# A hybrid diffusion layer on one core: tokens by quarters behind the heads, experts chosen during the merges, a regrouped gate matrix, and half of v split ahead

## The chip, the core and the metric

The kernel is one program on one core of a Trainium2 chip. The metric is the device time of one execution in microseconds, median of several runs. A core has TensorE (matmuls, PE in the profile; PEld its weight loads), VectorE (DVE), ScalarE (ACT), GpSimd (POOL) and SyncE (SP). Each works through its own instructions in order. DMAs are issued from the queues of SP, ACT and GpSimd and are carried by 16 shared DMA engines.

## What is computed

A layer over 1024 latent tokens and 256 context tokens of width 1024: two bidirectional gated linear scans (8 HGRN2 heads, 4 GLA heads) with one input projection, a gated merge of the two, an output projection, and then PEER, a retrieval of 16 out of 16384 experts per token for each of 8 heads. Cut to what the change touches:

```python
y = sigmoid(m_hg) * y_hg + sigmoid(m_gla) * y_gla
x = x + mod[2] * (y @ w_o)
h = modulate(rmsnorm(x, norm_ffn_g), mod[3], mod[4])
q  = (h @ wq).reshape(-1, 8, 2, 128)
s1 = einsum("nhd,kd->nhk", q[:, :, 0], k1); s2 = einsum("nhd,kd->nhk", q[:, :, 1], k2)
v1, i1 = top_k(s1, 16); v2, i2 = top_k(s2, 16)
top_s, top_c = top_k(v1[..., :, None] + v2[..., None, :], 16)
expert = i1[top_c // 16] * 128 + i2[top_c % 16]
act = gelu(einsum("pd,ped->pe", h, u[expert]))
x = x + mod[5] * einsum("pe,ped->pd", softmax(top_s) * act, v[expert])
return rmsnorm(x, final_g)
```

## The kernel before

Large products are made exact to about fp32 with two fp16 halves per operand: `split` (L91) writes the high half on ACT (L93) and the low half on DVE (L94), and `mm3` (L100) multiplies high by high, high by low and low by high. `ld` is a DMA on SP's queue, `st_` one on ACT's. The instructions' order on each engine is set by the order of the program text, in which generators are advanced by hand, and by a scheduler that moves loads ahead as far as their buffers allow.

*Heads* (to about 1460 us). Twelve heads are projected and scanned; the weight slabs come through three buffers (`w32`) that `slab` (L174) loads and splits. Beside them `presplit` (L311) splits weights of later stages and stores them in DRAM: 16 slabs of the two branch projections, 8 of the output projection, 16 of the query projection. `meanwhile` (L331) advances it by `PRE` = 0.25 units per 512 projected tokens. The merge gates (`w_m`) and the modulations (`mw`) come last.

*Merges* (1460 to about 1880). For each half of the tokens, 8 steps (`merge_step`, L818) multiply both branches by their weights, gate and add them (the addition on GpSimd) and split the result; `out_proj` (L833) gives x1, and `next_norm` (L871) normalises and transposes it into `hb`. In the second half's steps the generator `choosing(0)` (L764) is advanced by the table `CS`: `scores` (L739) multiplies by the query weights and the keys on PE, and DVE searches the best 16 (`top16`) of 128 twice per token block and head and then of 64 sums.

*Gating part* (1880 to 2858). Five token blocks (`DB` = 2, 3, 5, 6, 7) take the dense way: `route` turns the choice into expert numbers and gates on DVE, `gate_block` (L1051) builds for 4 tokens at a time one-hot matrices on DVE, multiplies them on PE and copies the result by ACT into `gs`; each 32 tokens the gate matrix `G_d` gets a store. The planner's price of each piece is what the generators yield (1.65 per 4 tokens, 16.0 a routing, 3.3 and 1.5 in choosing). Whenever the sum passes `U_US` = 6.2, `early_tile` (L1101) multiplies one tile of 128 experts' u with the dense tokens (transposes, `ph`), and stores the activations in `act_d`; 80 of 128 tiles are early. Each early tile also issues `G_E` = 3.4 gathers: the other three blocks (`GB` = 0, 1, 4) fetch their 128 chosen rows of u and then of v by indirect DMA from GpSimd (L940), and DVE uses each (L919, L924), 768 in all, six held in flight. They start once two blocks are routed, which `prep` does first.

*Expert loop* (to 4180). 32 groups of 4 expert tiles: the group's gates are loaded (`gt4`), activations are loaded or computed (`u_act`), `weigh` multiplies and splits them, `v_tile` (L1144) loads and splits v, and `out_unit` (L1151) multiplies for each of the five blocks; DVE adds the product to `acc` (L1162). The gathers left are fed in evenly. Then comes the final norm.

## Time and profile before

| | us |
|---|---|
| runs shown (3), lowest, median, highest | 4216.97, 4217.43, 4219.64 |
| profiled execution, its own time | 4229.67 |
| its span, first to last instruction | 4228.0 |
| PE busy (matmuls) | 3884.8 (92%) |
| DVE busy | 2938.6 (70%) |
| ACT busy | 1430.1 (34%) |
| GpSimd busy | 1683.9 (40%) |
| DMA, mean rate | 209 GB/s |

Busy time is the time in which at least one instruction of the engine ran; matmuls are pipelined, so a group's mean duration is longer than the distance between two of them. The granted clock is TensorE's, as a share of full speed. The idle time before an instruction is put down to what released it last.

### The profile page before, as it was taken

The numbers are of one execution on the slowest core, as the hardware profiler recorded it, in microseconds if no ns is written. First come the engines' busy times: TensorE is split into PE (matmuls) and PEld (weight loads), VectorE is DVE, ScalarE is ACT, GpSimd is POOL, SyncE is SP. The second block draws the span as 40 slices with busy tenths as digits, with TensorE's granted clock in tenths as the row PEclk, the third lists the DMA queues.
The fourth block names the chain that finished last, engine by engine and source line by source line (L and its number), as shares of the span: only waits on it lengthen the run. The fifth ranks groups of instructions, "written<-read, shape, count | busy, mean of one in ns | idle before, by whom it ended". The sixth has DMA issues, their size and how long they took to land.

```text
span 4228.0 us, 60334 instructions
## 1 busy us (share of the span) xinstructions
PE 3884.8 (92%) x23802; PEld 2350.2 (56%) x23802; DVE 2938.6 (70%) x5132; ACT 1430.1 (34%) x2194; POOL 1683.9 (40%) x1197
## 2 busy tenths in 40 slices
PE   6999999999999999988999989986899989999997
PEld 2665665656655444445776667763445544444453
DVE  5345446242556414379987799977989999889998
ACT  5344444243343202034543334552222222222222
POOL 2011111010011012127655567635766666666663
PEclk9999999999999999999999999987999999999998
DMA  5222122221223583227887778869989999989996
GB/s 189 78 73 85 56 73 79 74 87 46 87 64 115 162 282 107 99 97 242 295 307 249 254 242 298 305 228 319 329 318 336 321 323 325 316 311 325 328 315 232
DMA packets 435306, 884.64 MB, mean 209 GB/s; under 512 B 28511, under 2 KB 245066, under 8 KB 431438
## 3 DMA queue, kind: packets, MB, share of 16 engines
q0 software_dynamic: 110592, 402.70, 27.3%
q1 hardware_dynamic: 202676, 320.19, 22.6%
q10 hardware_dynamic: 121754, 157.89, 10.6%
q8 instruction: 186, 3.05, 0.3%
q14 instruction: 98, 0.80, 0.1%
HBM read 764.80 MB, written 115.88 MB: 208 GB/s over the span
## 4 chain that ended last, share of the span: by engine, by line
PE 47%; DVE 25%; DMA 11%; issue 8%; ACT 6%; POOL 4%; SPq 0%; ACTq 0%; DVEq 0%; POOLq 0%
PE ph L100 5%; DVE row_False L919 5%; PE pe L100 5%; DVE gacc L924 4%; PE pgm L1065 3%; PE pq L100 3%; PE pj_f0h L100 3%; PE pv_g L100 2%; PE pv_h L100 2%; DMA row_False<-in_peer_u_dram,idx 2%; PE pj_f1h L100 2%; PE pj_m L100 2%; DMA vn<-in_peer_v_dram 2%; DMA acr<-act_d 2%; PE pso L100 2%
## 5 line engine op out<-in xcount | busy, mean ns | idle before, releaser
L100 PE MATMUL pe<-v,w 128*128 128x512 f16 x3840 | 883.8, 392 | 138.7 <-DVE acc L1162 104.7
L100 PE MATMUL ph<-hb,uT 128*128 128x256 f16 (+1 forms) x6144 | 892.2, 303 | 14.6 <-POOL uT L967 10.4
L100 PEld LDWEIGHTS <-uT 128*128 128x128 f16 x6144 | 609.4, 99 | 242.5 <-POOL uT L967 13.1
L100 PEld LDWEIGHTS <-w 128*128 128x128 f16 x3840 | 384.0, 100 | 623.0 <-issue 166.4
L940 POOL DMA_INDIRECT row_False<-in_peer_u_dram,idx x384 | 548.9, 1429 | 274.6 <-DVE row_False L919 169.2
L940 POOL DMA_INDIRECT row_True<-in_peer_v_dram,idx x384 | 503.6, 1311 | 264.1 <-DVE gacc L924 173.1
L924 DVE SCALAR_TENSOR_TENSOR gacc<-row_True,dots,gacc 128x1024 f32<-128x1024 f32 x381 | 539.7, 1416 | 39.4 <-DMA row_True<-in_peer_v_dram,idx 35.8
L919 DVE SCALAR_TENSOR_TENSOR row_False<-row_False,h2n 128x1024 f32<-128x1024 f32 x384 | 496.2, 1326 | 67.1 <-DMA row_False<-in_peer_u_dram,idx 66.7
L967 POOL TENSOR_TENSOR uT<-uf,uT 128x512 f16<-128x512 f32 x256 | 380.8, 1499 | 284.0 <-ACT uf L966 282.6
L93 ACT ACTIVATE v<-vn 128x1024 f16<-128x1024 f32 x128 | 135.1, 1055 | 501.9 <-DMA vn<-in_peer_v_dram 386.7
L979 ACT ACTIVATE ac<-ph 128x256 f32<-128x256 f32 (+1 forms) x256 | 110.1, 438 | 371.8 <-PE ph L100 367.1
L1065 PE MATMUL pgm<-oh 128*128 128x128 f16 x1280 | 176.4, 295 | 53.2 <-ACT gs L1066 38.8
L1066 ACT ACTIVATE gs<-pgm 128x512 f32<-128x512 f32 x160 | 171.0, 1069 | 136.6 <-PE pgm L1065 136.6
L94 DVE SCALAR_TENSOR_TENSOR v<-vn,v 128x1024 f16<-128x1024 f32 x128 | 168.2, 1314 | 50.5 <-ACT v L93 50.3
L1162 DVE TENSOR_TENSOR acc<-pe,acc 128x1024 f32<-128x1024 f32 x155 | 188.6, 1217 | 11.8 <-PE pe L100 11.7
L100 PE MATMUL pj_m<-hb,w_m 128*128 128x512 f16 x768 | 187.4, 401 | 2.3 <-DVE lf_g L86 1.6
L1065 PEld LDWEIGHTS <-oh 128*128 128x128 f16 x1280 | 145.7, 117 | 77.0 <-issue 63.5
L100 PE MATMUL pq<-hb,w_wq 128*128 128x512 f16 x768 | 180.0, 387 | 1.0 <-POOL hb L89 0.8
L964 ACT ACTIVATE uT<-put 128x512 f16<-128x512 f32 x256 | 155.0, 605 | 71.0 <-PE put L961 69.4
L89 DVE TENSOR_TENSOR oh<-iota,rTr 128x1024 f16<-128x1024 f16 x160 | 139.1, 879 | 33.9 <-PE pgm L1065 33.8
L100 PEld LDWEIGHTS <-hb 128*128 128x128 f16 x1536 | 150.2, 98 | 17.8 <-issue 0.3
L966 ACT ACTIVATE uf<-put 128x512 f32<-128x512 f32 x256 | 154.4, 603 | 8.9 <-POOL uT L967 8.8
(364 smaller groups left out, 5531.9 us busy)
## 6 DMA issues: line engine op xcount, KB each, us to landing
un<-in_peer_u_dram SPq DMA_DIRECT2D x128, 512.0 KB
vn<-in_peer_v_dram SPq DMA_DIRECT2D x128, 512.0 KB
G_d<-gs ACTq DMA_DIRECT2D x20, 2048.0 KB
gt<-G_d ACTq DMA_DIRECT2D x32, 1280.0 KB
act_d<-ac ACTq DMA_DIRECT2D x80, 320.0 KB
acr<-act_d SPq DMA_DIRECT2D x80, 320.0 KB
mw<-in_ada_w_dram SPq DMA_DIRECT2D x32, 512.0 KB
w_wq<-wq_d SPq DMA_DIRECT2D x32, 512.0 KB
```

The lines of the kernel that those rows point to most:

```text
L89: eng.tensor_tensor(out=out, in0=in0, in1=in1, op=op)
L94: return V.scalar_tensor_tensor(out=lo, in0=src, scalar=float(scale), in1=hi, op0=ALU.mult, op1=ALU.subtract)
L100: PE.matmul(ps, lhsT=a(k), rhs=b(k), start=n == 0, stop=n == last)
L919: V.scalar_tensor_tensor(out=row, in0=row, scalar=1.0, in1=h2n, op0=ALU.mult, op1=ALU.mult, accum_out=dots[:, s:s + 1])
L924: V.scalar_tensor_tensor(out=gacc[n], in0=row, scalar=dots[:, s:s + 1], in1=gacc[n], op0=ALU.mult, op1=ALU.add)
L940: G.indirect_dma_start(out=row, out_offset=None, in_=src[0], in_offset=bass.IndirectOffsetOnAxis(ap=gsel[n][0][:, s:s + 1], axis=0))
L964: S.activation(hi, pv, AF.Copy, scale=SU)
L966: S.activation(uf, pv, AF.Copy, scale=SU)
L967: pace[0] = G.tensor_tensor(out=lo, in0=uf, in1=hi, op=ALU.subtract)
L1065: PE.matmul(pgm[:, t, :], lhsT=oh[:, 0, :, t], rhs=oh[:, j, :, t], start=j == 2, stop=j == 3)
L1066: S.activation(gs[:, :, t0:t0 + TB].rearrange("p i n -> p n i"), pgm, AF.Copy, scale=SA / SG)
L1162: vmark[0] = V.tensor_tensor(out=acc[n], in0=ps, in1=acc[n], op=ALU.add)
```

## The change

- *Quarters.* Tokens pass the merges by quarters of 256. The first and second quarter are merged alone, the third and fourth together with one load of the branch weights. The first quarter's output projection and norm stand behind the second and the fourth step of the second quarter's merges, the second quarter's norm behind the second step of the pair. The additions of the gated branches and of x1 go from GpSimd to DVE.
- *Choosing.* `choosing` takes a range of blocks. Blocks 0 and 1 are chosen from the fifth step of the second quarter on, then routed, then blocks 2 and 3, all inside the merges. `route` moves out of the gating part into a function before it. In `prep` remain the second half's choosing, the routing of block 4, and the five dense blocks. Gathers may start with the first early tile.
- *Pace.* `U_US` 6.2 to 6.8, `G_E` 3.4 to 3.6. Early tiles that do not fit in the gating part (`rest`) are computed in the loop's first group.
- *Gate matrix.* `G_d` is laid out by groups of 4 tiles, so that a group's load is one piece of 10 KB per partition; the store of 32 tokens is cut in 32 pieces of 512 bytes per partition.
- *v.* `presplit` runs only from the fifth head on (`late_heads`), at `PRE` = 0.84, stores through SP's queue, and gets 64 more units: the rows of v of the even expert tiles are split and stored in `v_d`. In the loop an even tile is loaded in two halves.

```diff
-U_US = 6.2
-G_E = 3.4
-CS = ((4, 4, 4, 4, 4, 4, 3, 3), (1, 1, 1, 1), 1, 0)
+U_US = 6.8
+G_E = 3.6
+QT = 2 * P
+CS = (5, 5, 10)
...
-PRE = 0.25
+NPRE = 64
+PRE = 0.84
...
-    G_d = dram.tile([TD // NB, P, P, NB], F32, name="G_d")
+    G_d = dram.tile([NKEY // GR, P, TD // NB, GR, NB], F32, name="G_d")
...
+            def rows(src, dst, sc, nm):
+                w32 = wi.tile([P, D], F32, name=f"w32_{nm}", tag="w32", bufs=3)
+                ld(out=w32, in_=src)
+                w16 = ws.tile([P, 2, D], F16, name=f"w16_{nm}", tag="w16", bufs=3)
+                split(w32, w16[:, 0], w16[:, 1], sc)
+                ld(out=dst, in_=w16)
...
-                    st_(out=br_d[bi * KC + j], in_=slab(w[0], j * P, f"pb{bi}{j}", SW))
+                    ld(out=br_d[bi * KC + j], in_=slab(w[0], j * P, f"pb{bi}{j}", SW))
...
+            for e in range(NPRE):
+                rows(v_r[2 * e], v_d[e], SV, f"v{e}")
+                yield
...
-            owed_[0] += PRE * w
+            owed_[0] += PRE * w * late_heads[0]
...
         for h in range(8):
+            late_heads[0] = h > 3
...
-            tt(G, rr[0], rr[0], rr[1], ALU.add)
+            for q in qs:
+                tt(V, rr["g", q], rr["g", q], rr["h", q], ALU.add)
+                split(rr["g", q], yTs[q][:, j, 0, :], yTs[q][:, j, 1, :], CM)
...
-                    tt(G, xt[:, cs], xt[:, cs], tm, ALU.add)
+                    tt(V, xt[:, cs], xt[:, cs], tm, ALU.add)
...
+        def first_half():
+            yield from choosing(0, 2, pp)
+            for n in (0, 1):
+                picks[n] = route(n)
+                yield 14.0
+            yield from choosing(2, 4, pp)
...
+        for j in range(KC):
+            merge_step((1,), j, yins, yTs)
+            if j == 1:
+                tiles = out_proj(0, yTs[0])
+            elif j == 3:
+                next_norm(0, tiles)
+            elif j > 3:
+                go(CS[0])
+        tiles = out_proj(1, yTs[1])
...
+            merge_step((2, 3), j, yins, yTs)
+            if j == 1:
+                next_norm(1, tiles)
+            go(CS[1])
+        tiles = [out_proj(q, yTs[q], lambda: go(CS[2] // 2)) for q in (2, 3)]
+        for q in (2, 3):
+            next_norm(q, tiles[q - 2])
+            go(CS[2])
...
-            st_(out=G_d[DB.index(n) * (P // NB) + nb], in_=gs)
+            st_(out=G_d[:, :, DB.index(n) * (P // NB) + nb].rearrange("g k a n -> k g (a n)"),
+                in_=gs.rearrange("k (g a) n -> k g (a n)", a=GR))
...
-            for n in (0, 1):
-                route(n)
-                yield 16.0
-            sel = route(2)
-            yield 16.0
-            yield from gating((2, 3), sel)
-            yield from choosing(1, ppg, lambda: route(4))
-            sel = route(5)
-            yield 16.0
-            yield from gating((5, 6, 7), sel)
+            yield from choosing(4, 8, ppg, fifth)
+            picked(4, picks.pop(4))
+            sel = route(DB[0])
+            yield 16.0
+            yield from gating(DB, sel)
...
-                if len(gsel) > 1:
-                    gathers(G_E)
-        while pend is not None:
-            early_tile()
+                gathers(G_E)
...
+        if e % 2 == 0:
+            ld(out=v16, in_=v_d[e // 2])
+            return v16
...
-            st_(out=gt4, in_=G_d[:, :, g * GR:(g + 1) * GR, :].rearrange("b i j n -> i b j n"))
+            st_(out=gt4, in_=G_d[g])
...
+                if g == 0:
+                    for r in rest[2 * j:2 * j + 2] if j < GR - 1 else rest[2 * j:]:
+                        st_(out=act_d[early.index(r)], in_=next_act(r))
```

Two places show how instructions move. The first is SP's queue in the second GLA head (`w32_gg`, `w32_kg`, `w32_qg`, `w32_vg` are slabs of the heads, `w32_pq` query weights to be split ahead, `w32_v9` a row of v, `v_d<-w16_v9` the store of its halves). Before:

```order
L179 DMA w32_gg0_0_7295<-in_w_in_dram 128x8x128
L179 DMA w32_gg0_1_7357<-in_w_in_dram 128x8x128
L179 DMA w32_pq5_7388<-in_peer_wq_dram 128x8x128
L179 DMA w32_kg2_7701<-in_w_in_dram 128x8x128
L179 DMA w32_pq6_7784<-in_peer_wq_dram 128x8x128
L179 DMA w32_qg2_7791<-in_w_in_dram 128x8x128
L380 DMA w32_vg20_7850<-in_w_in_dram 128x8x128
L380 DMA w32_vg21_7854<-in_w_in_dram 128x8x128
L179 DMA w32_pq7_7959<-in_peer_wq_dram 128x8x128
```

With the change:

```order
L180 DMA w32_gg0_0_7416<-in_w_in_dram 128x8x128
L320 DMA v_d_85<-w16_v8_7254 128x2048
L317 DMA w32_v9_7447<-in_peer_v_dram 128x1024
L317 DMA w32_v10_7481<-in_peer_v_dram 128x1024
L180 DMA w32_gg0_1_7490<-in_w_in_dram 128x8x128
L320 DMA v_d_85<-w16_v9_7449 128x2048
L317 DMA w32_v11_7521<-in_peer_v_dram 128x1024
L320 DMA v_d_85<-w16_v10_7483 128x2048
L317 DMA w32_v12_7555<-in_peer_v_dram 128x1024
L180 DMA w32_kg2_7840<-in_w_in_dram 128x8x128
L320 DMA v_d_85<-w16_v11_7523 128x2048
L317 DMA w32_v13_7897<-in_peer_v_dram 128x1024
```

Between the second gate slab and the next head's key slab there is one load to be split ahead in the first list; in the second there are two loads and two stores, and each store has to wait for the halves that it stores.

The second place is ACT's queue where the gating part ends and the loop begins (`gs7_3` the last 32 tokens' gates, `gt0` the first group's, `uT`, `uf` and `ac` the turning and the activations of a u tile, `CAST w16_0` the first half of the first weighted activations). Before:

```order
L1066 ACTIVATE gs7_3_24807<-pgm7_124_24902 128x4x128
L1068 DMA G_d_80<-gs7_3_24807 128x4096
L1180 DMA gt0_24949<-G_d_80 128x20x128
L93 ACTIVATE v16_0_24955<-vn0_24953 128x1024
L93 ACTIVATE v16_1_25041<-vn1_25039 128x1024
L1180 DMA gt1_25193<-G_d_80 128x20x128
L1140 CAST w16_0_24959<-acr0_24951 128x640
L93 ACTIVATE v16_2_25076<-vn2_25074 128x1024
L93 ACTIVATE v16_3_25165<-vn3_25163 128x1024
```

With the change:

```order
L1109 DMA G_d_80<-gs7_3_26381 128x32x128
L1072 ACTIVATE ac119_26594<-ph1_119_26621 128x384
L1057 ACTIVATE uT122_26689<-put122_0_26690 128x512
L1145 DMA act_d_81<-ac119_26594 128x640
L1238 DMA gt0_26677<-G_d_80 128x2560
L1059 ACTIVATE uf122_0_26696<-put122_0_26690 128x512
L1057 ACTIVATE uT122_26689<-put122_1_26699 128x512
L1059 ACTIVATE uf122_1_26705<-put122_1_26699 128x512
L1072 ACTIVATE ac120_26708<-ph0_120_26709 128x256
L1072 ACTIVATE ac120_26708<-ph1_120_26735 128x384
L1057 ACTIVATE uT1_26764<-put1_0_26765 128x512
L1179 CAST w16_0_26684<-acr0_26679 128x640
```

Behind the last gate store there stood two halves of v and the cast that needs `gt0`; now the rest of early tile 119, the activations of tile 120 and the turning of tile 122 stand there, and the cast behind them.

## Rows read from the trace of the kernel before

**Rows 1.** The page, head: busy time, share of the span, instructions.
```profile
PE 3884.8 (92%) x23802; PEld 2350.2 (56%) x23802; DVE 2938.6 (70%) x5132; ACT 1430.1 (34%) x2194; POOL 1683.9 (40%) x1197
```

**Rows 2.** Busy time by stretch; PE, weight loads, DVE, ACT, POOL, granted clock, DMA, GB/s.
```profile
60.00:1345.00 1285.00, 1231.56 (x8340) 782.04 (x8342) 620.17 (x1018) 515.20 (x724) 183.30 (x101) 0.98 0.25 75
1345.00:1460.00 115.00, 110.40 (x673) 59.33 (x670) 60.62 (x110) 21.57 (x34) 0.00 (x0) 0.96 0.50 156
1460.00:1880.00 420.00, 391.49 (x1838) 185.60 (x1836) 165.28 (x809) 62.58 (x109) 62.48 (x57) 0.97 0.43 147
1880.00:2140.00 260.00, 233.93 (x1717) 180.72 (x1718) 243.64 (x441) 130.60 (x208) 166.51 (x119) 0.97 0.74 260
2140.00:2480.00 340.00, 334.73 (x2298) 232.32 (x2297) 273.98 (x1004) 124.40 (x231) 190.33 (x162) 1.00 0.76 265
2480.00:2791.00 311.00, 279.38 (x2066) 219.28 (x2065) 295.02 (x337) 154.17 (x242) 220.67 (x153) 0.96 0.82 293
2791.00:2858.00 67.00, 47.49 (x357) 39.19 (x354) 38.06 (x48) 36.98 (x47) 9.51 (x8) 0.79 0.39 153
2858.00:2915.00 57.00, 23.19 (x101) 11.02 (x102) 35.99 (x52) 13.97 (x20) 27.54 (x18) 0.65 0.92 312
2915.00:4180.00 1265.00, 1164.88 (x6185) 617.29 (x6184) 1150.45 (x1248) 327.71 (x509) 821.91 (x573) 0.96 0.91 320
4180.00:4228.00 48.00, 26.64 (x109) 11.10 (x107) 39.24 (x42) 12.49 (x25) 0.94 (x1) 0.80 0.52 205
```

**Rows 3.** Waits of PE, 2915 to 4180: us in total, times, longest.
```profile
PE pe L100 <- DVE acc L1162: 98.3, 25, 9.1
```

**Rows 4.** Groups of DVE by line and shape, 2915 to 4180: v's low half.
```profile
L94 DVE SCALAR_TENSOR_TENSOR v<-vn,v 128x1024 f16<-128x1024 f32 x123 | 162.1, 1318 | 30.1 <-ACT v L93 30.0
```

**Rows 5.** Timeline of PE behind the last gating matmul.
```profile
2877.97 1.46 PE L100 MATMUL pe<-v,w 128*128 128x512 f16 x3 [20.40 <-ACT w L1140]
```

**Rows 6.** Tile act_d: stores, their issue in ns, first and last start.
```profile
L1105 ACTq DMA_DIRECT2D act_d<-ac x80: 325/326/362, 1893.3 to 2791.1; - x80
```

**Rows 7.** Tile w_m: ns min/median/max, first and last start in us.
```profile
L100 PEld LDWEIGHTS <-w_m x768: 95/98/182, 876.5 to 1476.3; 128*128 128x128 f16 x192
...
L179 SPq DMA_DIRECT2D w_m<-in_w_in_dram x16: 367/379/388, 827.0 to 1441.2; - x16
L93 ACT ACTIVATE w_m<-w_m x16: 1039/1056/1072, 838.5 to 1447.0; 128x1024 f16<-128x1024 f32 x16
L94 DVE SCALAR_TENSOR_TENSOR w_m<-w_m,w_m x16: 1207/1224/1226, 839.5 to 1448.1; 128x1024 f16<-128x1024 f32 x16
```

**Rows 8.** Groups of PE by line and shape, 60 to 725.
```profile
L100 PE MATMUL pv_h<-wv_h,hb 128*128 128x256 f16 x768 | 84.5, 273 | 0.2 <-ACT q_h L563 0.2
L100 PE MATMUL pj_f1h<-hb,w_f1h 128*128 128x512 f16 x384 | 84.2, 379 | 0.0
```

**Rows 9.** Tile pso: its addition on DVE.
```profile
L89 DVE TENSOR_TENSOR tm<-pso,mod x16: 690/691/693, 1574.8 to 1804.5; 128x512 f32<-128x512 f32 x16
```

**Rows 10.** Timeline of PE, one early tile between its transposes.
```profile
1890.31 1.04 PE L961 MATMUL put<-ident,un 128*128 128x128 f32 x8
...
1897.70 1.04 PE L961 MATMUL put<-ident,un 128*128 128x128 f32 x8
```

**Rows 11.** Groups of DVE by shape, 1880 to 1960: choosing's second search.
```profile
L760 DVE FIND_INDEX8 ii<-vv,wk 128x8 uint32<-128x128 f32 x8 | 2.2, 288 | 0.0
```

**Rows 12.** The same, 1880 to 2858: gathered rows in use.
```profile
L924 DVE SCALAR_TENSOR_TENSOR gacc<-row_True,dots,gacc 128x1024 f32<-128x1024 f32 x127 | 190.8, 1503 | 35.0 <-DMA row_True<-in_peer_v_dram,idx 34.1
L919 DVE SCALAR_TENSOR_TENSOR row_False<-row_False,h2n 128x1024 f32<-128x1024 f32 x131 | 176.6, 1376 | 44.6 <-DMA row_False<-in_peer_u_dram,idx 44.5
```

**Rows 13.** DMA queue of ACT, 2915 to 4180, then 1950 to 2860: packets, MB, share.
```profile
q10 hardware_dynamic: 74827, 38.07, 10.7%
...
q10 hardware_dynamic: 13408, 64.36, 18.1%
```

**Rows 14.** What SP's queue waited for, whole span.
```profile
SPq L179 <- DVE w_pq L94: 164.7, 12, 39.5
```

More of the change, by code (lines that the diff above doesn't have):

```diff
@@ L845, in out_proj, with h2_rows @@
                     tt(V, tm, ps, mod2[:, cs], ALU.mult)
-                    tt(G, xt[:, cs], xt[:, cs], tm, ALU.add)
+                    tt(V, xt[:, cs], xt[:, cs], tm, ALU.add)
                 st_(out=x1_d[n * P:(n + 1) * P, :], in_=xt)
                 tiles.append(xt)
-                if fill is not None:
-                    for _ in range(CS[1][i]):
-                        next(fill, None)
-            return tiles
-        def h2_rows(hf):
-            own = [n - hf * 4 for n in GB if n // 4 == hf]
-            o = sum(n // 4 < hf for n in GB)
+                then()
+            return tiles
+        def h2_rows(q):
+            own = [n - 2 * q for n in GB if n // 2 == q]
+            o = sum(n // 2 < q for n in GB)
+            if not own:
+                return None
             def rows_of(k, yt):
-                pt = pp.tile([P, 512], F32, name=f"ptr{hf}_{k}", tag="tr")
+                pt = pp.tile([P, 512], F32, name=f"ptr{q}_{k}", tag="tr")
                 w = len(own)
@@ L880, in tile_layer, with go @@
+        picks = {}
+        def first_half():
[4 more added lines that the diff above has]
+            yield from choosing(2, 4, pp)
+        steps = first_half()
+        def go(n):
+            for _ in range(n):
+                next(steps, None)
+        new_yT = lambda q: mg.tile([P, KC, 2, QT], F16, name=f"yT{q}", tag="yT", bufs=2)
+        yins, yTs = {0: load_y(0)}, {0: new_yT(0)}
         for j in range(KC):
-            merge_step(0, j, yin, yT)
+            merge_step((0,), j, yins, yTs)
@@ L908, in tile_layer, with picked @@
     gsel = {}
+    def picked(n, sel):
+        idx = pq.tile([P, P], mybir.dt.int32, name=f"idx{n}")
+        vmark[0] = V.scalar_tensor_tensor(out=idx, in0=sel[:, 0], scalar=float(NKEY), in1=sel[:, 1], op0=ALU.mult, op1=ALU.add)
+        gate = pq.tile([P, P], F32, name=f"gate{n}")
+        tsc(V, gate, sel[:, 2], SA * SV, ALU.mult)
+        gsel[n] = (idx, gate)
     pace, vmark = [None], [None]
@@ L1112, in tile_layer @@
         t_, pend = 0.0, nxt
+        for n in (0, 1):
+            picked(n, picks.pop(n))
         gth = gathering()
@@ L1166, in tile_layer, with next_act @@
     live = [e for e in range(NKEY) if e not in early]
-    uT = u_turn(live[0], u_load(live[0]))
-    li = 0
+    rest = [pend, *es] if pend is not None else []
+    todo = []
+    for j in range(GR):
+        todo += [j] * (j in live) + rest[2 * j:2 * j + 2]
+    todo += rest[2 * GR:] + [e for e in live if e >= GR]
+    if not rest:
+        uT = u_turn(todo[0], u_load(todo[0]))
+    ahead_ = iter(todo[1:])
+    def next_act(e):
+        nonlocal uT
+        en = next(ahead_, None)
+        uTn = u_turn(en, u_load(en)) if en is not None else None
+        ac = u_act(e, uT)
+        uT = uTn
+        return ac
     work = lambda e: 2.1 if e in early else 9.5
```

237 lines of the change are left out of this document (108 added, 129 removed).

## The prediction

> **What bounds the kernel now.** I read the page's head first [rows 1]: TensorE's matmuls (PE) are busy for 3884.8 of 4228.0 us, so the change, which takes no arithmetic away, can win little more than the 343 us in which PE stands still, and what a higher granted clock shortens. Where those lie is read from the busy time by stretch [rows 2], cut at the kernel's own stages. The heads (60 to 1460) leave PE idle for 1285 - 1231.6 + 115 - 110.4 = 58 us. The merges (1460 to 1880) leave 28.5. The gating part (1880 to 2858) leaves 83, of which 19.5 fall in its last 67 us at a granted clock of 0.79. The way into the expert loop (2858 to 2915) leaves 34 of 57 at a clock of 0.65. The loop itself (2915 to 4180) leaves 100, with PE at 92%, VectorE (DVE) at 91% and the DMA engines at 0.91: three resources close together.
>
> Who holds whom in the loop is read from the waits there [rows 3]: 98.3 of PE's 100 us end with the DVE addition that empties a product's PSUM buffer, so DVE, which runs in order, is late; and DVE itself waits 30.0 us for ACT's half of the v split [rows 4]. The way in is read from the timeline of PE [rows 5]: after its last gating matmuls it stands still for 20.40 us, until 2877.97, when the loop's first weights come. The last early tile had been stored at 2791.1 [rows 6], so nothing was left to fill that time with.
>
> **The change, part by part.** I cost each stage against the profiled execution (span 4228.0, own time 4229.67; the median of the runs shown, 4217.43, is 12 us below) and carry the difference over to the median.
>
> *Heads.* 64 rows of v are split here, behind the 40 weight slabs, all of it now after the fourth head: 64 DVE operations of 1.32 us [rows 4] (84 us) and 64 ACT copies of 1.06 us [rows 7] (68 us), on a DVE that is busy for 620 of 1285 us. What could be late is a slab of the head's own weights, since every store of a split now stands on SP's queue, in front of later loads. Today a slab has much in hand: the sixteen merge-gate slabs have their DVE half started at 839.5 (first) and 1448.1 (last), and PE takes them at 876.5 and 1476.3 (the same rows), 37 and 28 us later. So I cost most of the new work at nothing; its cover is that lead and the idle half of DVE. The exception is the end. The order puts 13 of the 64 units behind the first of the 32 modulation loads, in about the stretch 1345 to 1460, where DMA is busy for 0.50 x 115 = 58 us. A unit moves 1.05 MB; at the loop's 320 / 0.91 = 352 GB/s that is 3.0 us, so 39 us more, 97 of 115, all through three buffers. I take 12 us there and 8 for the other 51 units: **+20**. The ends: 0 (the lead covers all), and +53 (PE's idle time of 60 to 1345 doubles).
>
> *Merges.* Quarters make each 512-column product two of 256 columns, with the weights loaded for each. That is nearly free: 768 products of 256 columns take 84.5 us (110 ns), 384 of 512 take 84.2 (219 ns) [rows 8]; 1152 pairs at 1 ns more are 1 us. The first quarter needs 8.4 MB of branch weights, 4.2 of output weights, 2.1 of gates and 2.1 of its tokens during 42 us of PE (half of the four groups of 44 us that 1460 to 1565 holds); 16.8 MB at 352 GB/s are 48 us, so +6. DVE is busy for 165 of the 420 us today. To it come the additions that leave GpSimd (16 of 512 columns and 32 of 256, 22 us at the 0.69 us that a DVE operation of 512 columns takes here [rows 9]), two routings (28 us by the planner's price) and the first half's choosing that now runs past 1880 (18 us, below): 233, fed in steps of one head, in which DVE and PE come out about even in the second quarter and PE has more in the pair of quarters. At the end two norms run with no choosing left beside them; today 1770 to 1880 is the stage's weak place, so +6. Together **+12**; the ends are -15 (half of the 28.5 us goes) and +45 (DVE sets the pace of the second quarter's four steps and the eight after).
>
> *Gating part.* The yields of one choosing sum to 167.6, those of the rest to 376 before; at 6.2 a tile the 80 early tiles ran out at 2791. Now they sum to 167.6 and 344, at 6.8: 24.6 and 50.6 tiles, so 75 run here and 5 are left for the loop. Choosing took 2140 to 2480 for 27 tiles, PE busy 334.7: 12.4 us a tile, of which 7.4 are the tile itself (transposes at 1890.31 and 1897.70 [rows 10]) and 5.0 the choosing. With 6.8 / 6.2 of the latter, 12.9, at the same 0.985 busy, 24.6 tiles take 322 us. Gating is DVE's: 243.6 + 295.0 us in the 571 us of the other two stretches, 53 tiles. Some of it is choosing that spilled past 1880: 8 of 64 second searches [rows 11], an eighth of the 274 - 27 x 4.9 = 142 us of DVE that a whole choosing takes beside its gathers, 18 us. The rest is 9.8 a tile. Of it 3.4 gathered rows at 1.44 [rows 12] are 4.9; the other 4.9 grow by 6.8 / 6.2 to 5.4, and 3.6 rows cost 5.2. So 10.6, at today's DVE share of 0.94: 11.3 us, for 50.6 tiles 571. Together 893 for today's 978: **-85**. Ends -105 (PE as dense as in choosing) and -45 (GpSimd's and ACT's waits, 83 us of PE idleness, stay whole).
>
> *Way in and loop.* DVE loses 64 x 1.32 = 84 us and six or so gathers (8 us) of 36.0 + 1150.5; ACT's half goes with it, and with it half of the 30 us that DVE waits for ACT. PE gains five tiles, 5 x 7.4 = 37, on 23.2 + 1164.9: 1225. The five tiles lie in the way in: in ACT's queue the rest of tile 119, tile 120 and the turning of tile 122 stand ahead of the first cast that needs the gate matrix. I take PE's waits for DVE at 30 us in place of 98 and the way in at 10 in place of 34: 1265 for 1322, **-57**. The ends: -90 (no waits and a better clock) and +37 (the waits stay whole, and the tiles come on top).
>
> *Gate matrix.* Loads of 512-byte pieces in the loop become 10 KB pieces, and the stores become 512-byte ones in the gating part. In the loop's ACT queue 38.07 MB of mostly such pieces hold 10.7% of 16 engines for 1265 us, 135 us; in the gating part 64.36 MB in long pieces hold 18.1% of 910 us, 165 us [rows 13]. Per MB that is 3.6 against 2.6 us: some 38 us of DMA time leave the loop, 42 enter gating, where the share is 0.74 to 0.82. I count it at 0 on both sides. The Trainium skill (DMA: Bandwidth & Descriptors, Specifications) puts full rate at 512 bytes and up; by that nothing moves here, and rival B below would deserve 0.19, not 0.15. The trace disagrees with it by those two rows.
>
> The tail is untouched. **Sum:** 20 + 12 - 85 - 57 = -110, from 4217 to **4107 us**.
>
> **The rivals.**
> A, *slower: SP's queue in the heads.* A store cannot start before its DVE half, and SP stands still until then; loads of 52 slabs lie behind. If the lead of 28 us goes, each slab shows its chain: 5.8 us from issue to ACT, then 1.06 and 1.22 [rows 7], 8 us in all. From 110 / 8 = 14 exposed slabs on the gain is gone; at half of the 52, +208, about 4315. For it: SP already waits 164.7 us for DVE's splits, up to 39.5 in one go [rows 14]. Against: PE waits for no split today. The Trainium skill (the same page, on the anatomy of one DMA) says that semaphore waits are taken by the issuing sequencer before dispatch; row and rule agree that SP blocks, and only the lead decides.
> B, *the loop is held by gathered rows and DMA, not by DVE's load.* DMA is at 0.91 and its bytes hardly fall; then the loop keeps its 1322 us: 4107 + 57 = 4164, or 4201 with the five tiles on top. Against: DVE waits for a landed row only briefly there.
> C, *merges bound by DVE*, at the upper end above: 4107 + 33 = 4140, and with the heads' upper end 4173.
> D, *the five tiles do not fill the way in*, because ACT's in-order cast waits for the gate matrix: +24, 4131, inside the forecast.
>
> **How the numbers follow.** Forecast (with D) 0.62, B 0.15, C 0.12, A 0.08, other losses 0.03. The forecast's own range is 4050 to 4150; with B and C the range is **4040 to 4195**, which leaves out A and a sum of all the good ends (about 3995). A measurement here tells 0.2%, 8 us, from no change. Faster holds the forecast, B's and C's greater part: 0.87; within 0.2% 0.05; slower 0.08.
>
> **What would show it.** Right: 'pe' waits for DVE 'acc' under 50 us in the loop; no idle stretch of 20 us between gating and loop; the gating part near 895 us; the heads ending within 20 us of 1460, and no PE wait on a split. Wrong: PE waiting for a w16 slab in the later heads (A); a loop of 1310 us or more with DVE idle for rows (B); merges over 450 us (C).

## The result and the profile after

The change makes the kernel **slower** by 1.3%: 4272.4 us median (4260.9 to 4281.4, 4 runs) against 4218.5 (4217.0 to 4226.9, 4 runs), a ratio of 1.0127 with a 95% interval of 1.0100 to 1.0154. The forecast was 4107 us, in 4040 to 4195.

The page's head of the changed kernel answers to [rows 1]. The profiled execution's own time is 4281.37 us, its span 4278.6:

```profile
PE 3910.7 (91%) x24954; PEld 2473.0 (58%) x24954; DVE 2968.1 (69%) x5276; ACT 1446.8 (34%) x2262; POOL 1613.8 (38%) x1189
```

PE stands still for 4278.6 - 3910.7 = 368 us, where it was 343, and is busy for 26 us more. Next comes the busy time by stretch (columns as in [rows 2]), cut at the changed kernel's own stages: heads in two parts, merges, gating, way in, loop, tail:

```profile
60.00:1345.00 1285.00, 1237.22 (x8328) 784.81 (x8328) 670.82 (x1057) 563.18 (x769) 188.28 (x101) 0.97 0.36 113
1345.00:1494.00 149.00, 132.46 (x761) 71.69 (x762) 85.45 (x133) 38.18 (x53) 0.43 (x1) 0.92 0.72 236
1494.00:1953.00 459.00, 395.19 (x2935) 293.20 (x2934) 245.48 (x1100) 82.59 (x183) 26.75 (x49) 0.93 0.53 177
1953.00:2879.00 926.00, 835.54 (x5979) 627.58 (x5978) 797.39 (x1689) 413.71 (x674) 570.57 (x427) 0.97 0.81 272
2879.00:2967.00 88.00, 69.97 (x462) 47.59 (x461) 43.68 (x56) 29.22 (x54) 43.98 (x33) 0.90 0.88 315
2967.00:4230.00 1263.00, 1172.55 (x6250) 624.82 (x6249) 1068.91 (x1173) 276.67 (x456) 782.13 (x572) 0.96 0.88 318
4230.00:4278.00 48.00, 26.69 (x112) 11.22 (x110) 39.84 (x42) 12.50 (x25) 0.94 (x1) 0.80 0.51 200
```

The loop's line is the one to stop at. VectorE's (DVE) busy time went from 1150 to 1069 us there [rows 2], as forecast, and PE's idle time only from 100 to 90. All kernels of this study are compared below by the same marks: the last load of w_m weights ends the heads, the first transposition of u the merges, the last gating product the gating part, the first copy into acc the way in, the last addition to acc the loop. Each line of such times comes from one profiled execution, and executions of one kernel differ by up to 30 us in all (the change's four by 20), so a few us in one stage tell nothing by themselves.

| us, profiled execution | heads | merges | gating | way in | loop |
|---|---|---|---|---|---|
| before | 1476.3 | 404.5 | 976.5 | 57.9 | 1299.7 |
| the change | 1494.4 | 458.3 | 926.5 | 87.7 | 1298.6 |
| forecast for the difference | +20 | +12 | -85 | -57 with the loop | |
| measured difference | +18 | +54 | -50 | +30 | -1 |

What replaced the loop's lost work is in the waits there. First PE's, DVE's and those of SP's queue from 2967 to 4200 or 4210 us (waited for: us in total, times, longest), to be read against [rows 3] and [rows 4]:

```profile
PE pe L102 <- DVE acc L1204: 86.9, 25, 6.5
DVE acr L91 <- DMA acr<-act_d: 92.4, 38, 6.8
DVE w L1180 <- ACT w L1179: 45.6, 45, 3.0
DVE row_False L1012 <- DMA row_False<-in_peer_u_dram,idx: 41.5, 20, 6.1
SPq L1186 <- PE pe L102: 518.4, 60, 26.4
SPq L1189 <- DVE v L96: 284.0, 58, 16.2
```

PE still waits 87 us for acc. DVE's split of v is halved in number (x60 where [rows 4] has x123) and waits 0.3 us for ACT instead of 30, but DVE now waits 92.4 us for acr, the stored activations, for which it waited 13.6 before. In the kernel before, from 2915 to 4180, that wait and the longest one of SP's queue (L1146 loads v into a staging buffer, `vn`) were:

```profile
DVE acr L89 <- DMA acr<-act_d: 13.6, 13, 2.2
SPq L1146 <- DVE v L94: 833.9, 118, 22.3
```

Now SP's queue has a wait that it did not have: line 1186, the load of a split v tile straight into its final buffer, waits 518 us for PE, because that buffer is free only when PE has finished the group that used it. The queue waited as long before, for DVE, so the sum of its waits is no sign by itself. The timeline of SP's queue shows what stands behind the load of v (start, duration, what, count):

```profile
3305.11 0.33 SPq L1045 DMA_DIRECT2D un<-in_peer_u_dram  x1
3305.49 1.32 SPq L1244 DMA_DIRECT2D acr<-act_d  x2
3325.22 1.61 SPq L1186 DMA_DIRECT2D v<-v_d  x2
3330.18 3.79 SPq L1189 DMA_DIRECT2D vn<-in_peer_v_dram  x2
3334.07 0.38 SPq L1045 DMA_DIRECT2D un<-in_peer_u_dram  x1
3334.50 0.42 SPq L1244 DMA_DIRECT2D acr<-act_d  x1
```

From 3306.8 to 3325.2 the queue issues nothing, and the next acr leaves at 3334.5, after v, vn and un. **Theory H** came from this: DVE's work was replaced by DVE's waits, because acr stands in SP's queue behind loads that wait for PE, and PE waits for DVE. Its rivals: the DMA engines and gathered rows hold the loop (R2, the prediction's B), or acr's three buffers do (R7). For the merges and the gating part I had separate guesses, tested on the way.

### The profile page after: what moved, and what is told of

The parts are those of the page before. It is cut to its first block, busy times and chain, and to the rows that moved or that the text cites. A ratio compares the mean times of both kernels' runs of the same rounds, so it can differ in the third digit from the quotient of the medians.

```text
span 4278.6 us, 63252 instructions
## 1 busy us (share of the span) xinstructions
PE 3910.7 (91%) x24954; PEld 2473.0 (58%) x24954; DVE 2968.1 (69%) x5276; ACT 1446.8 (34%) x2262; POOL 1613.8 (38%) x1189
## 4 chain that ended last, share of the span: by engine, by line
PE 51%; DVE 19%; DMA 13%; issue 7%; ACT 6%; POOL 3%; ACTq 1%; SPq 1%; DVEq 0%; POOLq 0%
PE ph L102 8%; PE pe L102 7%; DMA acr<-act_d 4%; DVE gacc L1017 3%; PE pq L102 3%; DVE row_False L1012 3%; PE pgm L1106 3%; DMA row_False<-in_peer_u_dram,idx 3%; PE pv_g L102 2%; PE pv_h L102 2%; PE pj_f1h L102 2%; PE pj_f0h L102 2%; PE pj_qh L102 2%; PE pso L102 2%; ACT gs L1107 2%
## 5 line engine op out<-in xcount | busy, mean ns | idle before, releaser
L1033 POOL DMA_INDIRECT row_False<-in_peer_u_dram,idx x384 | 513.1, 1336 | 274.5 <-DVE row_False L1012 173.7
L1017 DVE SCALAR_TENSOR_TENSOR gacc<-row_True,dots,gacc 128x1024 f32<-128x1024 f32 x381 | 548.9, 1441 | 34.4 <-DMA row_True<-in_peer_v_dram,idx 29.7
L102 PE MATMUL pq<-hb,w_wq 128*128 128x256 f16 (+1 forms) x1152 | 178.0, 311 | 1.3 <-DVE yt_m L88 1.3
L91 DVE TENSOR_TENSOR acr<-acr,gt 128x640 f32<-128x640 f32 x80 | 70.8, 899 | 124.6 <-DMA acr<-act_d 95.5
L1054 PE MATMUL put<-ident,un 128*128 128x128 f32 x1024 | 141.1, 278 | 16.4 <-ACT uf L1059 16.4
L91 DVE TENSOR_TENSOR oh<-iota,rTr 128x1024 f16<-128x1024 f16 x160 | 129.8, 825 | 34.4 <-PE pgm L1106 34.4
```

The lines of the kernel that those rows point to most:

```text
L91: eng.tensor_tensor(out=out, in0=in0, in1=in1, op=op)
L102: PE.matmul(ps, lhsT=a(k), rhs=b(k), start=n == 0, stop=n == last)
L1017: V.scalar_tensor_tensor(out=gacc[n], in0=row, scalar=dots[:, s:s + 1], in1=gacc[n], op0=ALU.mult, op1=ALU.add)
L1033: G.indirect_dma_start(out=row, out_offset=None, in_=src[0], in_offset=bass.IndirectOffsetOnAxis(ap=gsel[n][0][:, s:s + 1], axis=0))
L1054: PE.transpose(pt[:, k * P:(k + 1) * P], un[:, (q * 4 + k) * P:(q * 4 + k + 1) * P], ident)
```

## The experiments

Line numbers differ between kernels; the names tell the operations. The ratio given is to the kernel before, run on the same chip, with its 95% interval.

**e1: no v part.** The loop `for e in range(NPRE)` of the splits is emptied, and the branch for even tiles in v_tile is taken out.

> Left as the changed kernel, but v is split nowhere ahead: the heads split only the projection weights, and the loop loads and splits all 128 v tiles as the kernel before did. Theory H (in the loop, SP's loads of split v wait for buffers that PE frees, and the loads of gathered-in acr behind them come late; so the v part pays nothing in the loop): the loop, 1301 us from first to last accumulation, stays within 15 us; the last w_m weight load falls from 1494 to about 1476, the merges' first 100 us lose 15 to 25 more; total 4272 -> 4225 to 4245. Rival R1 (the v part does pay its 50 us in the loop, and the moved gathers or the five late tiles took it back): the loop grows by 40 or more, total 4265 to 4300.

Measured 4254.9 us, 1.0067 (1.0050 to 1.0084); heads 1465.9, merges 443.0, gating 923.7, way in 94.0, loop 1312.1. The v part brought the loop 13 us and cost 44 in the heads and merges. H's stage forecasts hold (the heads fell by more), the total fell by less, to 10 us above H's range; R1 falls. DVE's acr waits in the loop are 19.9 us here, as small as in the kernel before.

**e2: acr and un issued by ScalarE's queue.**

```diff
-                    ld(out=ac, in_=act_d[early.index(e)])
+                    st_(out=ac, in_=act_d[early.index(e)])
...
-        ld(out=un, in_=u_r[e])
+        (st_ if late_u[0] else ld)(out=un, in_=u_r[e])
```

`late_u` is set where the loop begins.

> The changed kernel with the loop's acr and un loads issued by ScalarE's queue, so that only v and vn loads stand on SP's. H: DVE's waits for acr (92.4 us, 38 times in the loop) fall under 30, PE's waits for acc (86.9) under 45, the loop from 1301 to 1240-1265, total 4205 to 4240. Rival R2 (the loop is held by the gathered rows and the DMA engines at 0.88, not by SP's order): the acr waits turn into waits for rows or gacc of the same size, PE's waits for acc stay over 75, total 4262 to 4282. Rival R3 (ScalarE's queue now blocks its own copies): ACT waits grow by over 40 us, total over 4272.

Measured 4272.7 us, 1.0094 (1.0063 to 1.0125), loop 1297.6, acr waits 84.4: a miss for H, and near to R2. But ScalarE's timeline shows that acr only changed the thing it stands behind. DVE had emptied the last of the three buffers by 3337.4; acr left at 3343.27, behind activations that wait for PE:

```profile
3340.21 0.60 ACT L1058 ACTIVATE uT<-put 128x512 f16<-128x512 f32 x1 [4.56 <-PE put L1055]
...
3343.26 0.38 ACT L1073 ACTIVATE ac<-ph 128x256 f32<-128x256 f32 x1 [0.99 <-PE ph L102]
3343.27 0.33 ACTq L1246 DMA_DIRECT2D acr<-act_d  x1
```

So the run could not tell H from R2. The lesson for the next ones: the load that waits must move away, not the load that is late.

**e3: quarters 0 and 1 merged as a pair**, `merge_step((0, 1), ...)` eight times, then both output projections; `CS = (5, 8, 10)`.

> The changed kernel with quarters 0 and 1 merged as a pair, as 2 and 3 are: one load of each branch weight for both, then both output projections; the choosing steps go 8 to each step of the second pair. H (the first quarter, with half the PE time per weight load, is DMA-bound at 0.85 and 298 GB/s): the stretch from the last pj_m to the first put falls from 458 by 20 to 40 us, the DMA share of 1530-1595 under 0.7, the clock there over 0.95; total 4235 to 4255. Rival R4 (what is slow there is the late modulations and left-over v splits of the heads, whatever the merges load): the stretch changes by under 10 us; total 4262 to 4282. Rival R5 (the choosing, now later, makes the end of the merges DVE-bound): the stretch grows, total over 4285.

Measured 4278.8 us, 1.0125 (1.0096 to 1.0154), merges 460.2: no change (R4). The profiled start still had the late modulations in it, so it was repeated as e9.

**e4: the splits begin in head 2**, `late_heads[0] = h > 1` for `h > 3`; in the order all 64 v units then stand ahead of the modulations' loads.

> The changed kernel with the splits ahead begun in head 2 instead of head 4, so that all 64 v units are issued before the modulations' loads and none stands behind them. H: the last w_m weight load goes from 1494 to 1474-1482 and the first 35 us of the merges lose their clock of 0.66: together 20 to 40 us off, total 4232 to 4252. Rival R6 (the 67 MB cost the same wherever they stand): heads' PE waits appear earlier, total 4262 to 4282.

Measured 4249.1 us, 1.0053 (1.0034 to 1.0073); heads 1478.8 (-16), merges 446.4 (-12), the rest as in the change. R6 falls: standing earlier, the units cost 23 us of the median less. They are not free even so: the heads are 13 us longer than in e1, which has no v part. The stretch around the border, first of the change, then of e4:

```profile
1494.00:1575.00 81.00, 51.89 (x395) 38.59 (x393) 23.27 (x42) 6.58 (x13) 0.00 (x0) 0.84 0.81 281
```

```profile
1345.00:1479.00 134.00, 129.42 (x779) 69.65 (x777) 67.88 (x118) 24.98 (x40) 0.43 (x1) 0.97 0.50 160
1479.00:1560.00 81.00, 60.44 (x459) 47.15 (x458) 17.27 (x39) 4.88 (x12) 0.00 (x0) 0.87 0.83 280
```

The end of the heads is back at a DMA share of 0.50 (0.72 in the change), and PE gains 8.5 us in the first 81 of the merges.

**e5: v loaded by ScalarE's queue**, on e4: `st_(out=v16, in_=v_d[e // 2])`. **e6: a buffer more for acr**, on e4: every second acr tile has a buffer of its own.

> As the run with the splits begun in head 2, but the split v tiles are loaded by ScalarE's queue, where the wait for PE's v buffers blocks ScalarE and no load of acr or un. (In the run with acr and un on ScalarE's queue the acr loads stood behind ScalarE's own waits for PE, so that run did not test SP's order.) H: DVE's waits for acr in the loop, 89 us in 39, fall under 35; the loop goes from 1298 to 1240-1270; total 4195 to 4225. Rival R7 (acr comes late because its three buffers are freed late, whatever the queue): acr waits stay over 70, the loop within 10 us of 1298, total 4240 to 4258.

> As the run with the splits begun in head 2, but every second acr tile of the loop has a buffer of its own beside the three that acr and ac share. R7 (buffers): acr waits fall from 89 us to under 50 and the loop by 15 to 40, total 4205 to 4235. H (SP's order): the acr loads are issued no earlier, since they stand behind the v loads; waits stay over 75, the loop within 8 us, total 4242 to 4258.

e5: 4238.0 us, 1.0026 (1.0009 to 1.0042), loop 1285.2, acr waits 67.5. e6: 4253.4, 1.0061 (1.0042 to 1.0080), loop 1305.1, acr waits 94.5. A buffer alone does nothing, so R7 falls. The queue does something, but less than H said: 12 us of the loop, where H had 28 to 58, and the intervals of e4 and e5 overlap.

**e7: DVE takes 8 of 1024 columns of each gathered row in the loop**, on e4.

> As the run with the splits begun in head 2, but in the loop VectorE takes 8 of the 1024 columns of each gathered row (the rows are still fetched, and waited for); the rest of the experts' work on three token tiles is left out. R8 (VectorE's own stream, its work and its waits in order, sets when acc frees PE's banks): PE's waits for acc fall from 96 us to under 25, the loop to 1205-1230. R2 (the DMA engines and the gathered rows hold the loop): the loop stays over 1265, and DVE waits for rows by over 300 us.

One run, 4141.2 us; loop 1198.5. The loop by stretch and its waits:

```profile
2930.00:4129.00 1199.00, 1171.73 (x6384) 631.07 (x6381) 594.98 (x1205) 286.25 (x475) 601.14 (x572) 0.99 0.89 343
```

```profile
DVE acr L91 <- DMA acr<-act_d: 245.9, 57, 11.3
PE pe L102 <- DVE acc L1207: 22.8, 17, 5.1
```

The rows are still fetched, at 343 GB/s, and the loop is 100 us shorter: the prediction's rival B (R2) falls, and DVE's own stream holds PE (R8). It also shows that a DVE wait costs nothing by itself: 246 us of acr waits do no harm when DVE has 600 us to spare.

**e8 and e12: the kernel before with the v part alone** (splits from head 2, its own merges, choosing, gate layout and pace); e8 loads v on ScalarE's queue, e12 on SP's.

> The kernel before with the v part alone: splits begun in head 2, 64 v tiles split in the heads, the loop loads them split on ScalarE's queue. H: heads +2 to +6, merges +0 to +8, the loop from 1300 to 1245-1275 as in the run on the changed kernel, total 4178 to 4215 against 4219 to 4224 of before. R7: the loop within 10 us of 1300, total 4220 to 4235.

> The kernel before with the v part alone, splits from head 2, and the split v tiles loaded by SP's queue as the change does (on ScalarE's it took 4211 us, loop 1274, acr waits 71). H (SP's order takes the gain): loop 1290-1302, total 4223 to 4240, SP's waits for PE over 400 us. R7 (the queue doesn't matter): loop 1268-1280, total 4205 to 4217.

e8: 4211.1 us, 0.9964 (0.9953 to 0.9975), loop 1273.7. e12: 4236.0, 1.0025 (1.0012 to 1.0038), loop 1303.5. One word of code makes 25 us: the same part is a gain on one queue and a loss on the other. SP's waits of e12, then of e8:

```profile
SPq L1157 <- PE pe L101: 476.0, 55, 25.3
SPq L1160 <- DVE v L95: 303.3, 58, 19.3
```

```profile
SPq L1160 <- DVE v L95: 793.0, 56, 31.1
SPq L962 <- PE put L971: 221.5, 30, 16.9
```

e8's queue is still held, now by vn and un, and acr still waits 71.2 us. That is what e13 takes up.

**e9: the pair again**, on e5. **e10: the pace of before**, on e5: `U_US = 6.2`, `G_E = 3.4`.

> The run with splits from head 2 and v on ScalarE's queue (4238 us; merges, from the last w_m weights to the first put, 442 us, way in 88, loop 1285), and quarters 0 and 1 merged as a pair. The earlier pair run had the late modulations in its way. H: the first 80 us of the merges, in which PE works 60, gain 10 to 15 since each weight load now serves 512 columns; merges 425-433, total 4222 to 4232. R4' (the start is held by what is loaded in all, tokens and weights, not by the weight loads per quarter): merges 438-446, total 4233 to 4245. R5: choosing later makes the end longer: merges over 450.

> The same base (splits from head 2, v on ScalarE's queue), with the pace of before: U_US 6.2 and G_E 3.4, by which all 80 early tiles lie in the gating part and none in the way into the loop. H (PE idles 90 us in the gating part, waiting for VectorE, and five tiles of 7 us fit into that): gating 926 to 926-940, way in 88 to 55-62, total 4205 to 4228. Rival R9 (each tile costs its time wherever it stands): gating 955-965, total 4233 to 4245.

e9: 4238.7 us, 1.0037 (1.0019 to 1.0055), merges 443.4, so pairing gives nothing (R4'). e10: 4236.7, 1.0028 (1.0017 to 1.0038), gating 962.2, way in 63.7: five tiles cost 36 us in one place and give 24 in the other (R9). H's guess, that the gating part's idle time would take them in, falls.

**e11: the gate matrix laid out as before**, on e5. **e15: grouped as in the change, act_d stored by SP's queue**, on e5: `ld(out=act_d[...], in_=ac)`.

> The same base with the gate matrix laid out as before. H (the layout is worth nothing, as its loads and stores lie beside other work): every stage within 6 us, total 4232 to 4244. Rival R10 (stores in 512-byte pieces load the DMA engines while the gating part needs them for gathers, and lose more than the loads gain): gating 926 to 905-918, loop +0 to +6, total 4220 to 4232. Rival R11 (the loads' gain in the loop is real): loop +10 to +25, total 4248 to 4262.

> The changed kernel with splits from head 2 and v on ScalarE's queue (gating 926 us, 4238 us), gate matrix grouped as in the change, but act_d is stored by SP's queue in the gating part, so that ScalarE issues only the gate stores there. H (the store behind a gate store of 4096 pieces stands 7 to 14 us at its issue, and ScalarE with it): no issue on ScalarE over 1 us, gating 905-912, total 4216 to 4228. Rival (the DMA engines' time for 512-byte pieces): gating 921-928, total 4232 to 4244. Rival (SP's queue blocks in its turn and un comes late): gating over 930.

e11: 4221.8 us, 0.9995 (0.9985 to 1.0004), gating 907.9, loop 1281.7. e15: 4215.2, 0.9983 (0.9970 to 0.9996), gating 904.2, loop 1289.3. Grouping the gates cost 18 us of the gating part, and putting another store on another queue gives them back with the grouping kept. So it is not the DMA engines' time for 512-byte pieces: R10 had e11's numbers right and its reason wrong. The tile act_d in the change (duration of the issue in ns, min/median/max) and ScalarE's timeline where it is worst:

```profile
L1145 ACTq DMA_DIRECT2D act_d<-ac x75: 326/326/14162, 1970.8 to 2882.5; - x75
```

```profile
2880.65 0.38 ACTq L1109 DMA_DIRECT2D G_d<-gs  x1
...
2882.53 14.16 ACTq L1145 DMA_DIRECT2D act_d<-ac  x1
2899.80 0.33 ACTq L1238 DMA_DIRECT2D gt<-G_d  x1
```

```profile
2900.83 2.10 PE L1054 MATMUL put<-ident,un 128*128 128x128 f32 x8 [11.46 <-ACT uf L1059]
```

The last line is PE's, which waits 11.46 us for ScalarE here. Elsewhere it is the copy of a gating product that comes late:

```profile
2354.53 1.04 ACT L1107 ACTIVATE gs<-pgm 128x512 f32<-128x512 f32 x1 [6.82 <-issue]
```

A gate store of 2 MB now goes in 4096 pieces of 512 bytes. A store issued on the same queue within 8 us behind it takes 1.4 to 14.2 us to issue instead of 0.33, and ScalarE stands still with it: nine times, 72 us together in the change (from 8.9 us behind it on, 0.33 again), and never over 1 us in the gating part before ([rows 6] have a longest issue of 362 ns) and in e11; in e15 no issue of ScalarE's there is over 1 us. The Trainium skill (Perfetto Trace Analysis, DMA Instruction — HWDGE) says that the issuing sequencer is free only when a transfer's descriptors have all been generated. The trace agrees only in part: the large store's own issue takes 0.38 us, and it is the next, small store that stands 14.16 us.

**e13: SP's queue carries acr alone**, on e8: the loop's vn and un go to ScalarE's queue too. **e14: acr is not loaded**, on e8.

```diff
-        ld(out=vn, in_=v_r[e])
+        st_(out=vn, in_=v_r[e])
...
-        ld(out=un, in_=u_r[e])
+        (st_ if late_u[0] else ld)(out=un, in_=u_r[e])
```

> The kernel before with the v part and v on ScalarE's queue (loop 1274 us, acr waits 71, 4211 us), and in the loop vn and un on ScalarE's queue too, so that SP's queue carries acr alone. H (acr is late because of what stands before it on SP's queue): acr waits under 25 us, loop 1240-1262, total 4180 to 4202. R7 (acr is late because its buffer is freed late): acr waits 55-80, loop 1265-1285. R3 (ScalarE blocks on vn and un and its casts come late): VectorE's waits for w over 60, the loop over 1290, total over 4222.

> The kernel before with the v part and v on ScalarE's queue (loop 1274 us), but the stored activations are not loaded in the loop: their place is taken by ones (left out: 26 MB of loads and the early tiles' share of the result). If the 71 us of acr waits hold the loop: it falls by 30 to 60 to 1215-1245, PE's waits for acc from 88 to under 50. If they only fill time that VectorE would spend waiting elsewhere: the loop within 12 us of 1274, waits for rows or for PE up by over 40.

e13: **4126.7 us, 0.9780 (0.9762 to 0.9798)**, loop 1200.9, acr waits 0. e14: one run, 4120.4, loop 1190.0. H, that acr is late because of what stands before it on SP's queue, is shown, and larger than it said (both loops are below the ranges expected): e13 wins nearly all that removing the load altogether does. The loop by stretch, first of e8, then of e13:

```profile
2913.00:4180.00 1267.00, 1179.80 (x6242) 623.71 (x6242) 1107.55 (x1206) 278.83 (x463) 783.90 (x571) 0.96 0.90 324
```

```profile
2912.00:4100.00 1188.00, 1150.83 (x6223) 616.24 (x6222) 1107.08 (x1202) 276.21 (x457) 786.69 (x572) 0.99 0.95 345
```

And PE's wait, of e8, then of e13:

```profile
PE pe L101 <- DVE acc L1175: 86.2, 27, 7.5
```

```profile
PE pe L101 <- DVE acc L1176: 32.6, 16, 7.4
```

DVE does as much work (1107 us in both stretches) in a loop that is 73 us shorter by the marks. The 71 us of acr waits and 54 of PE's waits are gone, and PE, which stops less, is granted 0.99 of its clock for 0.96; its busy time by the marks falls from 1184 to 1161 us. SP's queue now waits 779 us for acr's own buffer, where it waited 66 in e8: acr leaves as soon as the buffer is free. The DMA engines go to 0.95, so 0.91 had been no limit. ScalarE has 280 us of work and can wait: its casts wait 160 us for PE in place of 87, and DVE waits for them 34 us in place of 26.

**e16 to e18: what needs what.** The same three lines in the kernel before without the v part (vn and un moved), in the change with nothing else touched, and in the change with the late splits (e4) and the stores (e15) mended as well.

> The kernel before, no v part, with the loop's vn and un loads on ScalarE's queue and acr alone on SP's. H (both are needed: VectorE's 84 us of v splits and a queue that brings acr in time; before, acr waits are 13.6 us): loop 1275-1300, total 4200 to 4222. Rival (the queues alone make the gain): loop under 1230, total under 4155.

> The change as it stands, with the loop's v, vn and un loads on ScalarE's queue and acr alone on SP's, and nothing else. H: the loop falls from 1299 to 1200-1225, DVE's waits for acr from 92 to under 15, the other stages stay within 8 us; total 4272 -> 4172 to 4200. Rival (something of the change's own loop, its later start or its gathers, holds it): loop over 1260, total over 4230.

> The change with its three waits mended: splits from head 2, v, vn and un of the loop on ScalarE's queue, act_d stored by SP's queue. By stages: heads 1480, merges 442, gating 905, way in 86, loop 1200-1215, tail 13: 4122 to 4145, level with the kernel before plus the v part (4127), so that quarters and the moved choosing are worth nothing on the chip. Rival (they pay once nothing hides them): under 4115.

| | us | ratio | heads | merges | gating | way in | loop |
|---|---|---|---|---|---|---|---|
| e16 | 4265.3 | 1.0105 (1.0080 to 1.0129) | 1474.4 | 403.5 | 972.3 | 62.1 | 1340.7 |
| e17 | 4174.2 | 0.9885 (0.9866 to 0.9904) | 1490.0 | 460.8 | 929.9 | 85.7 | 1201.4 |
| e18 | 4129.8 | 0.9788 (0.9768 to 0.9808) | 1482.4 | 443.3 | 905.7 | 84.3 | 1197.2 |

e16 is slower than before, which I had not expected: there every v tile has its high half made by ScalarE, which now waits longer for vn, a load of its own queue, and DVE waits behind it. ScalarE's wait in the kernel before, then in e16:

```profile
ACT v L93 <- DMA vn<-in_peer_v_dram: 352.8, 62, 11.9
```

```profile
ACT v L93 <- DMA vn<-in_peer_v_dram: 406.2, 63, 17.0
```

And DVE's in e16, where [rows 4] have 30.0 us:

```profile
DVE v L94 <- ACT v L93: 68.6, 27, 5.0
```

By the marks PE's waits for acc rise from 104.7 to 137.6 us. So the gain needs both, half of the splits done ahead and a queue that brings acr in time. e17 changes nothing in the change but who issues three loads, and turns a loss of 1.27% into a gain of 1.15%. Of PE's 87 us of waits for acc in the loop and DVE's 92 for acr these are left:

```profile
PE pe L102 <- DVE acc L1205: 29.5, 15, 8.9
DVE acr L91 <- DMA acr<-act_d: 1.5, 2, 0.8
```

e18 is 2.1% faster than the kernel before, and e13 2.2%, which has none of the quarters, the moved choosing, the grouped gates and the five tiles; the two are not told apart (0.9788 and 0.9780, intervals overlapping). Together those parts are worth nothing here: e18's merges, gating part and way in take 1433 us, e13's 1437.

## Why the prediction was wrong

*Heads, +20:* right in size (+18) and, in the main, in place (the units behind the modulations). It is put together otherwise: from 60 to 1345 PE did nearly the same work in both kernels, so the 8 us for the other units did not come, and the end cost all 18 in place of 12. That the sum is so near is in part luck. Not seen: the same units go on costing in the merges. Together they are 23 us, and e4 has them back.

*Merges, +12:* the failed sizes are "16.8 MB at 352 GB/s are 48 us, so +6" and "1152 pairs at 1 ns more are 1 us". Measured +54, outside its own ends. The stage by its marks, before, then in the change:

```profile
1476.30:1880.80 404.50, 375.99 (x1761) 178.04 (x1760) 161.31 (x807) 61.14 (x106) 62.48 (x57) 0.97 0.43 146
```

```profile
1494.40:1952.70 458.30, 394.49 (x2931) 292.74 (x2930) 245.19 (x1099) 82.59 (x183) 26.75 (x49) 0.93 0.53 177
```

PE's busy time is 18.5 us more, where 1 was counted, and its idle time 35 more. Some 12 are the late units (e4); the other 40 stay in e4, e9 and e18, where the busy time is about that of the change and 20 of the 35 us of idle time are left. There the first quarters are slow. PE's groups by shape (busy us, mean ns, idle before), one branch's products in the second, the first and the last quarter of the change's merges:

```profile
L102 PE MATMUL pb_g<-yin1g,w_bg 128*128 128x256 f16 x192 | 25.4, 286 | 10.0 <-DMA w_bg<-br_d 10.0
L102 PE MATMUL pb_g<-yin0g,w_bg 128*128 128x256 f16 x192 | 24.7, 289 | 9.4 <-DMA yin0g<-yg_d 7.2 <-DMA w_bg<-br_d 1.4 <-DVE msg_g L888 0.7
...
L102 PE MATMUL pb_g<-yin3g,w_bg 128*128 128x256 f16 x192 | 22.3, 273 | 0.0
```

A product of this branch takes 129 to 132 ns in the first two quarters and 116 in the last, where I had put 110 [rows 8], and 19 us of waiting, nearly all for weights and tokens, stand ahead of them. PE's granted clock is 0.84 over the first 81 us (the row under e4), where the kernel before has 0.98 (1476 to 1557). Which of these the quarters need not pay stays open; pairing the first two took the wait for weights away (5.2 us for tokens and 10.4 for DVE are there instead) and did not shorten the stage.

*Gating part, -85:* measured -50, and -71 with the queues right (e18, 905.7). The failed step is the gate matrix: "I count it at 0 on both sides". I priced the pieces by the DMA engines' time, which e11 and e15 show to be no cost at all, and not by the engine that issues them. The rest of the arithmetic, tiles times a stretch's own time per tile, came within 14 us, helped by errors to both sides: in e18 the 26 tiles before the first gating product take 320 us, 12.3 each where 322 / 24.6 = 13.1 were forecast, and the 49 behind it 586, 12.0 each for 11.3.

*Way in and loop, -57:* measured +29, the step that turned the sign. What I expected of DVE's work was right; with the queue mended it is (85.7 + 1201.4) - (57.9 + 1299.7) = -70, and PE's waits for acc are 29.5 us (e17). The step that failed is that PE's waits would fall "at 30 us in place of 98" as soon as DVE had less to do; they were 87. Between the forecast's 1265 us and the 1351 of the two stretches above, 60 are PE's idle time in the loop (90 for 30), 8 its idle time in the way in (18 for 10) and 18 its busy time (1242.5 for 1225). I counted the work that left DVE's stream and not the wait that entered a queue's. A v tile's load used to wait for a staging buffer, now for PE, and behind it stood the load that DVE needs next. But v's own load is the smaller part: moved alone it won 12 us of the loop (e4 to e5), or 30 in the kernel before (e12 to e8), while e17, with vn and un moved too, won 97. Those two had stood in front of acr before the change as well, almost without harm. With half of the splits done ahead, a load of vn waits 14 us for its buffer where it waited 7 (793.0 us in 56 waits in e8, 833.9 in 118 before); that this is why they now make acr late is argued from these rows and not shown by a run of its own. DVE's in-order stream lost 81 us of work and gained as much in waits: its waits for acr, w, v and gathered rows were 97 us in the loop before and 181 after.

*The five tiles* fill the way in as forecast (PE 70 of 88 us busy, 23 of 57 in [rows 2]), but 30 us longer, and e10 shows that in the gating part they cost about as much (the totals, 4236.7 and 4238.0, are not told apart). So D did not come: PE's longest wait there is 11.5 us, where it was 20.4 [rows 5].

*The rivals.* A named the right mechanism, a wait at the head of SP's queue with the next loads behind it, and put it in the heads, where the lead of the slabs just covered it: from the last split of w_m to its last weight load it shrank from 28 to 12 us, and PE's weight loads waited 0.7 us for a split there. In the loop, where it struck, I never asked what was queued behind the moved load. B falls by e7 and e13: with DMA at 0.95 the loop is shorter by 73. C's sign, merges over 450 us, came true, but not by DVE's pace: DVE is busy for 245 of 459 us, and of PE's 64 idle us there 23 end with DVE, 11 of them with the late modulations. The chance of 0.08 for slower stood for one place of a mechanism that has as many places as queues. Three slips in the working move nothing: the sum of all the good ends is 4007 us, not 3995 (0 - 15 - 105 - 90 from 4217); the 42 us of PE in the merges are half of two groups (44.1 and 39.2 us from 1460 to 1565), not of four; and the lead of 28 us is counted to a slab's last use, while its first is 12 us earlier.

## What to carry to other kernels

When a load's destination changes, write down what frees the new destination, and then what stands behind that load on the queue that issues it: a load that waits for a buffer must not be in front of one that the engine on the critical path needs next. Work taken off an in-order engine is won only if its next operand is there sooner too, so look for the wait that will take the work's place. When a store is cut into smaller pieces, look at the engine that issues it, not only at the DMA engines.

## What the hardware showed that I had not expected

The choice of the issuing engine alone is worth 84 us here: 4211.1 us with v on ScalarE's queue and vn, un and acr on SP's, 4126.7 with acr alone on SP's (e8, e13). The Trainium skill (DMA: Bandwidth & Descriptors, Issuing engines are not separate DMA queues) says that starting DMAs on several engines saves only the time it takes to start them. For the bytes that holds here (324 GB/s at a DMA share of 0.90 in e8 and 345 at 0.95 in e13 are 360 and 363 per full share), but the waits ahead of a start are what counts, and the measurement decides.

A store's issue can take 14.16 us in place of 0.33 when it follows a store of 4096 pieces on the same queue, and the engine does no other work meanwhile.

The loop of e13 ran at a DMA share of 0.95 and 345 GB/s with PE idle for 37 of 1188 us; 0.91 and 320 GB/s [rows 2], which I had called one of three resources close together, was no bound.
